# Four leading units instead of two after each sub-layer boundary, and all low parts of the weights on VectorE

## The chip, the cores and the metric

The kernel runs on one core of one Trainium2 chip. The metric is the device time of one launch in microseconds (us). A run is one execution; the time before is the median of three runs, and one more execution was profiled. The core has a matrix engine (PE, with a separate queue PEld for loading the stationary operand), VectorE (DVE), ScalarE (ACT), GpSimd (POOL) and SyncE (SP, which here only issues DMA transfers). Each engine works off its own instructions in order and waits on semaphores for the others.

## The reference

One layer of a hybrid decoder is applied to 512 prompt tokens and 8 single-token samples, 520 token columns in all, with a model width of 1024. Norms cross all three sub-layers:

```
x = x + 0.5 * rmsnorm(swiglu(rmsnorm(x, g1), gate1, up1, down1), post1)     # first feed-forward, hidden 2816
m, states  = token_mixer(rmsnorm(x, gm), ...)                                # mixer
x = x + rmsnorm(m, postm)
x = x + 0.5 * rmsnorm(swiglu(rmsnorm(x, g2), gate2, up2, down2), post2)     # second feed-forward
swiglu(x)  = (silu(x @ gate) * (x @ up)) @ down
token_mixer: proj = h @ w_in; retention branch (4 heads), gated delta branch (4 heads, short conv of width 4,
             chunks of 64, a triangular solve per chunk), y = sig(gr)*(o_r @ w_r) + sig(gg)*(o_g @ w_g); y @ w_out
```

Outputs are the new x of prompt and samples and the new retention, delta and conv states.

## The kernel before, in words

Activations are kept transposed: a tile `x[k]` holds 128 channels (k = 0 to 7) by 520 tokens. Every matmul takes a 128x128 piece of a weight as stationary operand and 260 tokens (a half, `HALVES`) as moving operand. Full float32 accuracy comes from three passes over float32r parts (`passes`, L298 to L300): high part of the weight times high part of the activation, high times low (`xl`), low times high. A weight's high part `whi` is a cast by ACT (L258), its low part `wlo` the difference raw minus `whi` (L259). `split_x` does the same for activations: ACT writes the high part (L389), DVE the low part (L390), both in a tile `xhl`.

A **unit** is the weight of one output tile of 128 channels: 8 pieces k. A unit over both halves is 8 x 3 x 2 = 48 matmuls; it is one product `product`. Plain pairs of the feed-forwards (`g` for gate, `u` for up) are two units each, `PLAIN` = 3 of them in each feed-forward; the other 19 pairs (m from 3 to 21) are computed in seven products of half depth and half the tokens each (`seven`, tile `sv`), 84 matmuls where a plain pair has 96, from combined weights (`s1`, `s3`, `a22` with sums made by DMA) and combined activations (`token_factors`). Their order is the table `stream`. `hidden` turns a plain pair into a hidden tile: `t` = g * r on DVE (L617), silu on ACT (L621), product on DVE, and the split of it.

The program is written in the order in which the engines execute it. Side tasks are Python generators (`spawn`); each `yield n` gives the main stream of PE work n steps (`tick`) before the task emits its next instructions. So a number in a `yield` sets how many matmuls stand on PE between two steps of a chain. `next_unit` hands out the next split weight and calls `prefetch`, which emits the split of units to come (two ahead) as buffers come free; `hold` stops that while x is being prepared.

At a boundary between sub-layers the following happens. The last output tile `dn` of the sub-layer is done half by half (`down`, `staged`). `post` for a half takes the sum of squares (PE `ss`, L360), the inverse root (POOL `pow`, L355), spreads it over the partitions (PE `rb`, L366), then for each k DVE makes `t` = y * rb (L492), POOL adds it to x (L494), ACT and DVE split x. So the next sub-layer's PE work can start on half 0 as soon as the first `xhl` is there. The inverse root of the new x (`pre_rms`) needs both halves; ACT squares x (L407), DVE adds the squares over k (`add_squares`, L435), then `inverse_rms` makes `ss`, `rs`, and `rb` for both halves. It isn't needed by the products themselves, which are scaled by r after the matmul, but by what reads them.

`two_first` takes the first two units together: at half 0, k by k, both units, then the same at half 1; the half 0 result of the first is copied out of PSUM (`early`). Then come units 2 and 3 over both halves each. The first units of the mixer are GAB (gates), CK, CQ, CV of head 0, of the second feed-forward the gate and up of pairs 0 and 1. `urgent` units (number 2) are split in four pieces; `on_pool` units, and every odd unit in the mixer while `share_split` is set, have their low part made on POOL rather than DVE (30 in all).

## Time and profile before

| | us |
| --- | --- |
| median of three runs | 1298.24 |
| lowest and highest | 1297.49, 1301.72 |
| the profiled execution's own time | 1299.34 |
| its span (first to last instruction) | 1297.3 |
| PE busy, mean granted clock | 1233.3, 0.962 |
| DVE, ACT, POOL busy | 866.5, 547.0, 317.2 |

What lies outside the span is 2.0 us. In the profile, L numbers are lines of the kernel before; an entry such as `[2.18 <-ACT whi L258]` behind an instruction says that its engine was idle for 2.18 us before it and what released it. Times of places are counted from the start of the span: the first feed-forward ends and the mixer begins at about 379 us, the second feed-forward begins at about 892 us.

### The profile page before, as it was taken

What the parts mean: (1) busy time and instruction counts of PE and PEld (TensorE: products, weight loads), DVE (VectorE), ACT (ScalarE), POOL (GpSimd) and SP (SyncE); (2) the same over time, 40 slices, a digit from 0 to 9 for tenths busy, and PEclk for the clock granted to TensorE, in tenths of its full rate; (3) what the DMA queues carried; (4) which work ended last, traced back from release to release, by engine and by line L of the source; (5) the groups of instructions that cost most, each with busy time, mean ns of one, the idle gap of its engine ahead of it and who ended that gap; (6) DMA issues with size and microseconds to landing.
All of it is one profiled execution on the core that took longest, in us unless ns stands there. A gap on an engine that the chain in (4) does not pass through costs nothing.

```text
span 1297.3 us, 25497 instructions
## 1 busy us (share of the span) xinstructions
PE 1233.3 (95%) x10061; PEld 1219.7 (94%) x10061; DVE 866.5 (67%) x1911; ACT 547.0 (42%) x1127; POOL 317.2 (24%) x410
## 2 busy tenths in 40 slices
PE   8899999999998997999999999998889999999995
PEld 7899999999988997989999999998889999999995
DVE  8888888642254887877687655446768887862334
ACT  6566655522233553212333343323546655542220
POOL 4111211000024359227512333403311111100003
PEclk8999999999997999899999999997889999999997
DMA  5677777243321233232333564321377777634321
GB/s 172 170 182 195 177 185 178 86 156 92 97 62 53 95 101 89 71 101 97 106 133 111 178 205 136 126 82 50 119 192 183 180 196 182 147 90 156 90 74 66
DMA packets 77127, 167.38 MB, mean 129 GB/s; under 512 B 14544, under 2 KB 20016, under 8 KB 77008
## 3 DMA queue, kind: packets, MB, share of 16 engines
q1 hardware_dynamic: 64432, 140.95, 33.9%
q0 software_dynamic: 12576, 24.81, 10.9%
q8 instruction: 79, 1.29, 0.4%
q14 instruction: 40, 0.33, 0.1%
HBM read 156.03 MB, written 9.70 MB: 128 GB/s over the span
## 4 chain that ended last, share of the span: by engine, by line
PE 71%; DVE 11%; POOL 5%; issue 4%; DMA 4%; ACT 3%; SPq 1%; POOLq 0%; ACTq 0%; DVEq 0%
PE sv L298 10%; PE sv L299 10%; PE sv L300 10%; PE dn L299 7%; PE dn L298 7%; PE dn L300 7%; PE p L298 4%; PE p L300 4%; PE p L299 4%; DVE wlo L259 2%; DMA s<-gu_in 2%; DVE cv L1048 1%; PE br L298 1%; PE br L299 1%; PE br L300 1%
## 5 line engine op out<-in xcount | busy, mean ns | idle before, releaser
L298 PE MATMUL p<-xhl,whi 128*128 128x260 f32 x784 | 237.5, 303 | 2.2 <-ACT whi L258 2.2
L300 PE MATMUL p<-xhl,wlo 128*128 128x260 f32 x784 | 227.8, 291 | 1.8 <-DVE wlo L259 1.0
L299 PE MATMUL p<-xhl,whi 128*128 128x260 f32 x784 | 228.3, 291 | 0.7 <-DVE xhl L390 0.6
L299 PE MATMUL dn<-hl,whi 128*128 128x260 f32 x704 | 199.6, 283 | 3.3 <-DVE hl L606 3.3
L298 PE MATMUL dn<-hh,whi 128*128 128x260 f32 x704 | 199.5, 283 | 0.0
L300 PE MATMUL dn<-hh,wlo 128*128 128x260 f32 x704 | 198.8, 282 | 0.0
L298 PE MATMUL sv<-th,w 128*128 128x260 f32 x608 | 173.2, 285 | 4.4 <-ACT u L638 4.3
L299 PE MATMUL sv<-tl,w 128*128 128x260 f32 x608 | 172.9, 284 | 0.0
L300 PE MATMUL sv<-th,w 128*128 128x260 f32 x608 | 172.9, 284 | 0.0
L298 PEld LDWEIGHTS p<-xhl,whi 128*128 128x128 f32 x784 | 154.5, 197 | 3.1 <-ACT whi L258 2.4
L259 DVE TENSOR_TENSOR wlo<-raw,whi 128x1024 fp32r<-128x1024 f32 (+2 forms) x107 | 116.4, 1105 | 60.4 <-ACT whi L258 60.0
L300 PEld LDWEIGHTS p<-xhl,wlo 128*128 128x128 f32 x784 | 154.1, 197 | 2.3 <-DVE wlo L259 1.2
L299 PEld LDWEIGHTS p<-xhl,whi 128*128 128x128 f32 x784 | 154.3, 197 | 1.6 <-DVE xhl L390 1.1
L258 ACT CAST whi<-raw 128x1024 fp32r<-128x1024 f32 (+2 forms) x137 | 126.7, 943 | 65.5 <-DMA raw<-dn_in 55.2
L218 POOL DMA_DIRECT2D s<-gu_in x76 | 67.1, 954 | 322.6 <-DMA s<-gu_in 149.1
L277 DVE TENSOR_TENSOR w<-s,w 128x512 fp32r<-128x512 f32 x152 | 104.5, 689 | 53.2 <-ACT w L276 52.1
L299 PEld LDWEIGHTS dn<-hl,whi 128*128 128x128 f32 x704 | 132.6, 188 | 4.1 <-DVE hl L606 4.1
L298 PE MATMUL sv<-xhl,w 128*128 128x260 f32 x456 | 129.4, 284 | 4.2 <-DVE t L617 4.2
L300 PEld LDWEIGHTS dn<-hh,wlo 128*128 128x128 f32 x704 | 132.6, 188 | 0.0
L298 PEld LDWEIGHTS dn<-hh,whi 128*128 128x128 f32 x704 | 132.6, 188 | 0.0
L299 PE MATMUL sv<-xhl,w 128*128 128x260 f32 x456 | 129.0, 283 | 0.0
L300 PE MATMUL sv<-xhl,w 128*128 128x260 f32 x456 | 128.9, 283 | 0.0
(362 smaller groups left out, 2990.8 us busy)
## 6 DMA issues: line engine op xcount, KB each, us to landing
raw<-gu_in SPq DMA_DIRECT2D x49, 512.0 KB, 3.7
raw<-win_in SPq DMA_DIRECT2D x49, 512.0 KB, 3.5
s<-gu_in SPq DMA_DIRECT2D x76, 256.0 KB, 4.2
s<-gu_in POOLq DMA_DIRECT2D x76, 256.0 KB, 4.8
raw<-dn_in SPq DMA_DIRECT2D x32, 448.0 KB, 3.5
a<-gu_in SPq DMA_DIRECT2D x38, 256.0 KB, 4.6
raw<-dn_in SPq DMA_DIRECT2D x16, 512.0 KB, 3.6
x<-x SPq DMA_DIRECT2D x16, 260.0 KB, 6.3
```

What stands on the lines that cost most here:

```text
L218: self.nc.gpsimd.dma_start(out=out, in_=term, accum_op=ALU.add)
L258: self.nc.scalar.copy(hi[:, ks], t[:, ks])
L259: eng.tensor_tensor(lo[:, ks], t[:, ks], hi[:, ks].bitcast(F32), ALU.subtract)
L277: nc.vector.tensor_tensor(w[:, 1], t[i], w[:, 0].bitcast(F32), ALU.subtract)
L298: mm(ps, hi[:, k, :], xh, start=first, stop=False, skip_group_check=more)
L299: mm(ps, hi[:, k, :], xl, start=False, stop=False, skip_group_check=more)
L300: mm(ps, lo[:, k, :], xh, start=False, stop=last, skip_group_check=more)
L1048: nc.vector.scalar_tensor_tensor(out=acc, in0=cin[:, j : j + SEQ], scalar=w[:, j : j + 1], in1=acc, op0=ALU.mult, op1=ALU.add)
```

## The change

The diff does five things.

1. In mixer and second feed-forward, four units lead (`first_units` with groups (0,1) and (2,3)) where `two_first` had two: half 0 of units 0 and 1 interleaved over k, half 0 of units 2 and 3, then the same at half 1. The half 0 results of all are copied out by ACT. The first feed-forward keeps two units, one behind the other.
2. All low parts are made on DVE; `on_pool`, `share_split` and `urgent` are gone.
3. In `post`, the split of unit 1 is emitted behind the second `t` of half 0, and those of units 2 and 3 behind the last `xhl` of half 0. The squares are added once, 520 wide, after half 1 (seven additions in place of fourteen half as wide), `inverse_rms` waits for the first group's half 1 and one step, and its spread comes four steps behind the root instead of two.
4. The second feed-forward has four plain pairs, so one pair fewer in sevens.
5. In both feed-forwards the `hidden` of the last plain pair is spawned when the stream is at its fourth product (n == 3), no longer ahead of the stream.

On PE, around the start of the mixer, the order before was the following (rows are the first matmul of each turn of a tile; `p` are the projection's PSUM tiles, and the operand in the middle tells the unit, `whi_4692` unit 0, `whi_4912` unit 1, `whi_5101` unit 2):

```order
L298 MATMUL p_4908<-xhl_4837,whi_4692 128x260 [waits Activation_49]
L298 MATMUL p_4918<-xhl_4837,whi_4912 128x260 [waits Activation_49]
...
L360 MATMUL ss_4939<-ones,acc_638_3487 65x1 x4
...
L366 MATMUL rb_4977<-cst,rs_4946 128x65 [waits Pool_49]
...
L298 MATMUL p_5020<-xhl_5003,whi_4692 128x260 [waits Activation_49]
L298 MATMUL p_5024<-xhl_5003,whi_4912 128x260 [waits PE_49]
...
L298 MATMUL p_5127<-xhl_4837,whi_5101 128x260 [waits Activation_49]
L298 MATMUL p_5128<-xhl_5003,whi_5101 128x260 [waits PE_49]
L360 MATMUL ss_5135<-ones,sq_4820 65x1 [waits PE_49]
```

And it is now (`whi_4692`, `whi_4826`, `whi_4971`, `whi_4977` are units 0 to 3):

```order
L294 MATMUL p_4908<-xhl_4849,whi_4692 128x260 [waits Activation_49]
L295 MATMUL p_4908<-xhl_4849,whi_4692 128x260 [waits DVE_49]
L296 MATMUL p_4908<-xhl_4849,wlo_4693 128x260
L294 MATMUL p_4912<-xhl_4849,whi_4826 128x260
...
L294 MATMUL p_5020<-xhl_4849,whi_4971 128x260 [waits Activation_49]
L294 MATMUL p_5024<-xhl_4849,whi_4977 128x260 [waits PE_49,Activation_49]
...
L294 MATMUL p_5123<-xhl_5015,whi_4692 128x260 [waits Activation_49]
...
L356 MATMUL ss_5187<-ones,sq_4832 65x1 [waits DVE_49]
```

Half 0 of units 2 and 3 (`p_5020`, `p_5024`) has moved ahead of the first matmul of half 1 (`p_5123`), and the sum of squares `ss_5187` stands 60 matmuls further from it: 48 of half 1 of units 0 and 1, and 12 of units 2 and 3.

On DVE at the same place, before and then now (`wlo` of unit 1 ahead of the fifth `t` to after the second, `t` and `xhl` are the pieces of half 0; `sq` the sums of the squares):

```order
L390 SCALAR_TENSOR_TENSOR xhl_4889<-x_3862,vec,xhl_4889 128x260 [waits Activation_49]
L401 TENSOR_TENSOR acc_638_3487<-acc_638_3487,s_4893 128x260 [waits Activation_49]
L512 TENSOR_SCALAR y_4758<-dn_4763,gh 128x260
L259 TENSOR_TENSOR wlo_4913<-raw_4683,whi_4912 128x1024 [waits DMAHW0_49,Activation_49]
...
L390 SCALAR_TENSOR_TENSOR xhl_4954<-x_3865,vec,xhl_4954 128x260 [waits Activation_49]
L435 TENSOR_TENSOR sq_4820<-sq_4820,sq_4821 128x260
```

```order
L474 TENSOR_TENSOR t_4823<-y_3849,rb_4809 128x260
L255 TENSOR_TENSOR wlo_4827<-raw_4683,whi_4826 128x1024 [waits DMAHW0_49,Activation_49]
L474 TENSOR_TENSOR t_4846<-y_4026,rb_4809 128x260 [waits Pool_49]
L384 SCALAR_TENSOR_TENSOR xhl_4849<-x_3858,vec,xhl_4849 128x260 [waits Activation_49]
...
L384 SCALAR_TENSOR_TENSOR xhl_4961<-x_3865,vec,xhl_4961 128x260 [waits Activation_49]
L255 TENSOR_TENSOR wlo_4972<-raw_4696,whi_4971 128x1024 [waits DMAHW1_49,Activation_49]
L255 TENSOR_TENSOR wlo_4978<-raw_4830,whi_4977 128x1024 [waits DMAHW2_49,Activation_49]
```

The low part of unit 1 has moved ahead of the first `xhl`, and where the first seven additions of squares stood, the low parts of units 2 and 3 stand now.

On ACT at the start of the first feed-forward's stream (`s_775` is silu of the last plain pair, `u` and `q` copies of the stream's first results out of PSUM), before and now:

```order
L276 CAST w_139_761<-s_120_625 128x512 [waits PE_49]
L621 ACTIVATE s_775<-t_765 128x260 [waits DVE_49,Activation_49]
L621 ACTIVATE s_776<-t_766 128x260 [waits DVE_49,Activation_49]
L638 COPY u_779<-sv_751 128x260 [waits PE_49]
```

```order
L272 CAST w_139_761<-s_120_625 128x512 [waits PE_49]
L640 COPY u_770<-sv_751 128x260 [waits PE_49]
L272 CAST w_143_787<-s_142_785 128x512 [waits DVE_49,Activation_49]
L643 COPY q_790<-sv_772 128x260 [waits PE_49]
L272 CAST w_145_804<-a_105_535 128x512 [waits DMAHW2_49,Activation_49]
L646 COPY u_807<-sv_751 128x260 [waits PE_49]
L272 CAST w_150_826<-raw_532 128x512 [waits Activation_49]
L623 ACTIVATE s_831<-t_816 128x260 [waits DVE_49,Activation_49]
```

The two silu have moved behind three copies and three casts.

The diff:

```diff
@@ -37,7 +37,7 @@
 RAW_BUFS, SPLIT_BUFS, AHEAD = 2, 9, 2
 SUM_LAG = 6
 SLOTS = 68
-PLAIN = {1: 3, 2: 3}
+PLAIN = {1: 3, 2: 4}
 SPLIT_H = 10
 
 
@@ -127,9 +127,6 @@
         self.first_of = {}
         for j, g in enumerate(self.group):
             self.first_of.setdefault(g, j)
-        kinds = [u[0] for u in self.unit_list]
-        self.on_pool = {kinds.index("win") + n for n in (3, 4)} | {kinds.index("gu2") + 3}
-        self.urgent = {kinds.index("win") + 2, kinds.index("gu2") + 2}
         self.loaded = {}
         self.split_done = {}
         self.raw_next = self.split_next = self.use_next = 0
@@ -140,8 +137,8 @@
         self.rooted = False
         self.ahead = 0
         self.tasks = []
-        self.share_split = False
         self.hold = False
+        self.leads = 0
         self.now = 0
 
 
@@ -237,7 +234,7 @@
                 self.split_seven(j)
             else:
                 nk = self.unit_list[j][3] - self.unit_list[j][2]
-                self.split(j, [slice(z, z + 2) for z in range(0, nk, 2)] if j in self.urgent else [slice(0, nk)])
+                self.split(j, [slice(0, nk)])
             self.load_to(self.split_next)
 
     def started(self, j):
@@ -253,10 +250,9 @@
             self.started(j)
         t = self.loaded[self.group[j]]
         hi, lo = self.split_done[j]
-        eng = self.nc.gpsimd if j in self.on_pool or self.share_split and j % 2 else self.nc.vector
         for ks in parts:
             self.nc.scalar.copy(hi[:, ks], t[:, ks])
-            eng.tensor_tensor(lo[:, ks], t[:, ks], hi[:, ks].bitcast(F32), ALU.subtract)
+            self.nc.vector.tensor_tensor(lo[:, ks], t[:, ks], hi[:, ks].bitcast(F32), ALU.subtract)
 
     def split_seven(self, j):
 
@@ -368,13 +364,11 @@
             )
         return pb[:, 0:HC]
 
-    def rstd(self, acc, scale, wait, plus, meanwhile=None):
+    def rstd(self, acc, scale, wait, plus):
 
         ps = self.bank("ss")
         self.sums(ps, acc, PIECES)
         _, r = self.root(ps, PIECES, scale, plus)
-        if meanwhile is not None:
-            meanwhile()
         yield wait
         return self.spread(r)
 
@@ -417,22 +411,12 @@
                 while len(xs[hf]) <= k:
                     yield 1
                 self.square(k, hf, nc.scalar)
-            if hf == 0:
-
-                while not self.clear:
-                    yield 1
-                self.add_squares(0)
-        self.prefetch(True, 1)
-        self.add_squares(1)
-        yield 2
+        for k in range(1, KD):
+            nc.vector.tensor_tensor(sq[0], sq[0], sq[k], ALU.add)
+        while not self.leads:
+            yield 1
+        yield 1
         yield from self.inverse_rms(sq[0], r, plus)
-        self.hold = False
-
-    def add_squares(self, hf):
-        c0, n = HALVES[hf]
-        acc = self.sq[0][:, c0 : c0 + n]
-        for k in range(1, KD):
-            self.nc.vector.tensor_tensor(acc, acc, self.sq[k][:, c0 : c0 + n], ALU.add)
 
     def inverse_rms(self, acc, r, plus):
         nc = self.nc
@@ -442,7 +426,8 @@
         if plus is not None:
             nc.vector.tensor_scalar(plus[0:PW], m[0:PW], EPS, None, ALU.mult)
         self.rooted = True
-        yield 2
+        self.hold = False
+        yield 4
         out = self.wk.tile([P, TOK], F32, tag="rb", name=self.name("rb"), bufs=1)
         for hf, (c0, n) in enumerate(HALVES):
             pb = self.spread(s[:, hf * PIECES : (hf + 1) * PIECES])
@@ -460,11 +445,8 @@
         c0, n = HALVES[hf]
         cs = slice(c0, c0 + n)
         self.hold = self.hold_sums = gnext is not None
-        yield 1
-        meanwhile = (lambda: self.clear.append(1)) if hf else (lambda: self.prefetch(True, 1))
-        r2 = yield from self.rstd(
-            acc, 1.0 / D, 2 if gnext is None else 3, plus and plus[0:PW, hf * PIECES : (hf + 1) * PIECES], gnext is not None and meanwhile or None
-        )
+        yield 1 if gnext is None else 2
+        r2 = yield from self.rstd(acc, 1.0 / D, 2 if gnext is None else 3, plus and plus[0:PW, hf * PIECES : (hf + 1) * PIECES])
         if gnext is None:
             r2s = self.work("u", n)
             nc.scalar.copy(r2s, r2)
@@ -483,7 +465,7 @@
             return
         if not hf:
             self.rooted = False
-            self.clear = []
+            self.leads = 0
             self.spawn(self.pre_rms(xs, r, plus_next))
...
             if k >= lag:
                 xs[hf].append(self.split_x(k - lag, hf, gnext))
+            if not hf and k == 1:
+                self.prefetch(True, 1)
             yield 1
+        if not hf:
+            self.prefetch(True, 2)
 
 
     def down(self, xin, pieces, gpost, gnext, held, plus=None, plus_next=None, x_from=None):
@@ -531,19 +517,35 @@
         self.staged([job] * held, sum(pieces), xin, "dn", lambda j, hf, ps: evac(KD - held + j, hf, ps), False)
         return xs, r
 
-    def two_first(self, xs, name, by_k):
-
...
-        self.staged([lambda: [(self.next_unit(), range(KD))]] * 2, KD, xs, name, done, by_k)
+    def first_units(self, xs, name, groups):
+
+
+        n = sum(len(g) for g in groups)
+        ws, banks = [None] * n, [[None, None] for _ in range(n)]
+        early = [self.slot("early") for _ in range(n // 2)]
+        for hf, (c0, cols) in enumerate(HALVES):
+            for group in groups:
+                ps = {}
+                for k in range(KD):
+                    for j in group:
+                        if ws[j] is None:
+                            ws[j] = self.next_unit()
+                        while len(xs[hf]) <= k:
+                            self.tick()
+                        if j not in ps:
+                            ps[j] = self.dbank(name, cols)
+                        self.passes(ws[j], k, xs[hf][k], ps[j], k == 0, k == KD - 1)
+                    if len(group) > 1 or k % 2:
+                        self.tick()
+                for j in group:
+                    banks[j][hf] = ps[j]
+                    if hf:
+                        self.release()
+                    else:
+                        banks[j][0] = early[j // 2][:, j % 2 * HC : j % 2 * HC + cols]
+                        self.nc.scalar.copy(banks[j][0], ps[j])
+                if hf:
+                    self.leads += 1
         return banks
 
     def token_factors(self, xs, gcol, F):
@@ -680,15 +682,24 @@
             return banks, at
 
         self.spawn(self.token_factors(xs, gpre, F))
-        self.spawn(hidden(*self.two_first(xs, "g", x_from is not self.a["xT"])))
-        for m in range(1, plain):
+        lead = self.first_units(xs, "g", ((0,), (1,)) if x_from is self.a["xT"] else ((0, 1), (2, 3)))
+
+        def leads():
+            for j in range(0, len(lead), 2):
+                yield from hidden(*lead[j : j + 2])
+
+        self.spawn(leads())
+        for m in range(len(lead) // 2, plain):
             pg = self.product([(self.next_unit(), range(KD))], xs, "g")
             pu = self.product([(self.next_unit(), range(KD))], xs, "u")
-            self.spawn(hidden(pg, pu))
+            if m < plain - 1:
+                self.spawn(hidden(pg, pu))
         while r[0] is None or r[1] is None:
             self.tick()
         pairs = {}
-        for m, i in stream(plain):
+        for n, (m, i) in enumerate(stream(plain)):
+            if n == 3:
+                self.spawn(hidden(pg, pu))
             if m not in pairs:
                 pairs[m] = pair(m)
             banks, at = pairs[m]
@@ -825,30 +836,18 @@
         self.turn = 0
         self.gcol = None
         self.dec_done = set()
-        tiles, gate, lead = {}, {}, {}
+        tiles, gate, lead = {}, {}, []
 
         def project(kind, h):
-            if kind == GAB:
-                lead[GAB, 0], lead[CK, 0] = self.two_first(xs, "p", True)
-                return
-            if (kind, h) == (CK, 0):
-                return
-            ps = self.product([(self.next_unit(), range(KD))], xs, "p")
             if lead:
-                lead[kind, h] = ps
-                if len(lead) < 4:
-                    return
-                while r[0] is None or r[1] is None:
-                    self.tick()
-                self.spawn(self.gates(self.gate_rows(lead[GAB, 0])))
-                for kind in (CK, CQ):
-                    tiles[kind] = self.conv(lead[kind, 0], kind, 0)
-                lead.clear()
-                self.share_split = True
-                kind = CV
+                ps = lead.pop(0)
+            else:
+                ps = self.product([(self.next_unit(), range(KD))], xs, "p")
             if (kind, h) == (CK, 1):
                 self.spawn(positions())
-            if kind in (CQ, CK, CV):
+            if kind == GAB:
+                self.spawn(self.gates(self.gate_rows(ps)))
+            elif kind in (CQ, CK, CV):
                 tiles[kind] = self.conv(ps, kind, h)
                 if kind == CV:
                     self.spawn(self.gdn_head(h, tiles[CQ], tiles[CK], tiles[CV]))
@@ -878,6 +877,9 @@
 
                 self.spawn(tanh())
 
+        lead += self.first_units(xs, "p", ((0, 1), (2, 3)))
+        while r[0] is None or r[1] is None:
+            self.tick()
         for kind, h in proj_order()[: -2 * KD]:
             project(kind, h)
         yx, part = [[], []], []
...
```

More of the change, by code (lines that the diff above doesn't have):

```diff
@@ L532, in down @@
         return xs, r
-    def two_first(self, xs, name, by_k):
-        banks = [[None, None], [None, None]]
-        early = self.slot("early")
-        def done(j, hf, ps):
-            if j == 0:
-                c0, n = HALVES[hf]
-                self.nc.scalar.copy(early[:, c0 : c0 + n], ps)
-                ps = early[:, c0 : c0 + n]
-            banks[j][hf] = ps
-        self.staged([lambda: [(self.next_unit(), range(KD))]] * 2, KD, xs, name, done, by_k)
+    def first_units(self, xs, name, groups):
[25 more added lines that the diff above has]
+                    self.leads += 1
         return banks
```

1 line of the change is left out of this document (removed).

## The prediction

> **What bounds the kernel now.** I read the page first: engines and slices.
>
> ```profile
> PE 1233.3 (95%) x10061; PEld 1219.7 (94%) x10061; DVE 866.5 (67%) x1911; ACT 547.0 (42%) x1127; POOL 317.2 (24%) x410
> ...
> PEclk8999999999997999899999999997889999999997
> ```
>
> PE, busy 95% of the span, is the bound nearly everywhere. The clock row has a digit per slice of 32.4 us; behind the start it dips in the slices from 389, 519 and 876 to 940 us. There is time to win only where PE idles, and where its clock is below 1. So I asked for windows around the two boundaries (columns: stretch, length, busy us and count of PE, PEld, DVE, ACT, POOL, then granted clock, DMA share, GB/s):
>
> ```profile
> 379.15:429.70 50.55, 43.99 (x294) 42.44 (x293) 30.39 (x70) 18.59 (x42) 18.36 (x19) 0.80 0.17 53
> 379.80:383.20 3.40, 0.51 (x2) 0.30 (x2) 3.40 (x6) 3.40 (x8) 1.71 (x2) 0.98 0.00 0
> 383.00:390.00 7.00, 6.62 (x35) 6.62 (x35) 5.42 (x13) 1.06 (x3) 2.39 (x2) 0.51 0.25 77
> 400.10:403.50 3.40, 1.91 (x20) 1.82 (x19) 3.26 (x9) 1.12 (x4) 0.00 (x0) 1.00 0.29 42
> 403.50:417.20 13.70, 12.53 (x62) 12.53 (x63) 1.64 (x5) 2.27 (x3) 6.34 (x3) 0.50 0.17 68
> 411.50:429.70 18.20, 18.20 (x132) 18.02 (x132) 9.17 (x23) 4.28 (x6) 5.26 (x5) 0.84 0.27 88
> 429.70:480.00 50.30, 50.22 (x423) 49.96 (x422) 42.29 (x98) 31.94 (x81) 24.86 (x27) 1.00 0.35 107
> 480.00:580.00 100.00, 86.77 (x688) 84.53 (x686) 83.04 (x237) 29.10 (x69) 52.28 (x89) 0.91 0.29 88
> 891.80:938.90 47.10, 39.32 (x243) 37.59 (x242) 35.30 (x75) 23.41 (x52) 16.93 (x17) 0.75 0.25 80
> 895.00:908.70 13.70, 12.21 (x58) 11.91 (x59) 8.12 (x18) 2.67 (x6) 4.05 (x6) 0.50 0.10 40
> 922.30:932.60 10.30, 9.59 (x46) 9.33 (x45) 7.68 (x12) 5.30 (x11) 3.34 (x2) 0.50 0.17 58
> 938.90:954.60 15.70, 11.54 (x97) 11.33 (x95) 8.87 (x16) 4.51 (x9) 2.39 (x3) 0.95 0.86 235
> ```
>
> At full clock a matmul takes 50.22 / 423 = 0.119 us, so a unit of 48 takes 5.7 and four take 22.8. The first four units of the mixer take 50.55 us, those of the second feed-forward 47.1: 28 and 24 us more than their matmuls. Half of that is clock: 20.7 us at half speed in the mixer (10.3 lost), 24.0 in the feed-forward (12.0 lost). Each such stretch follows a few us in which PE was little busy (0.51 of 3.40, 1.91 of 3.40). What those stalls are, the waits of PE say (line, releaser, us in total, times, longest):
>
> ```profile
> PE cs L1370 <- DVE gsq L1482: 5.6, 1, 5.6
> PE ss L360 <- DVE sq L435: 5.3, 2, 2.7
> PE sv L298 <- ACT u L638: 4.3, 2, 3.4
> PE sv L298 <- DVE t L617: 4.2, 1, 4.2
> PE g L298 <- ACT whi L258: 3.4, 1, 3.4
> PE rb L366 <- POOL rs L355: 3.1, 3, 1.3
> PE p L298 <- ACT whi L258: 2.2, 1, 2.2
> ```
>
> Unit 1's split comes late (`whi`, 2.2 and 3.4), the sum of squares stands on the path (`sq`, twice 2.7).
>
> **Lead of the mixer.** The change gives PE 48 matmuls between the halves that need no new x, and puts unit 1's split ahead of the pieces. The pieces of x come at one per 0.90 us (xhl at 378.53, the next at 379.43):
>
> ```profile
> 378.53 0.60 DVE L390 SCALAR_TENSOR_TENSOR xhl<-x,vec,xhl 128x260 fp32r<-128x260 f32 x1
> 379.43 0.60 DVE L390 SCALAR_TENSOR_TENSOR xhl<-x,vec,xhl 128x260 fp32r<-128x260 f32 x1
> 950.90 0.69 DVE L571 TENSOR_TENSOR tl<-ta,th 128x520 fp32r<-128x520 f32 x1
> 405.99 1.64 POOL L355 TENSOR_TENSOR rs<-ms,mhalf 65x8 f32<-65x8 f32 x1 [7.11 <-DVE ms L351]
> L259 DVE TENSOR_TENSOR wlo<-raw,whi 128x1024 fp32r<-128x1024 f32 x59 | 73.3, 1242 | 13.4 <-ACT whi L258 13.2
> ```
>
> My walk: unit 1's `wlo` ahead of the first xhl, 1.2; half 0 of units 0 and 1 paced by x, 8 x 0.90 plus the last six matmuls, 7.9; a wait on the sums of half 1 and on `rb`, up to 2.7 together (rows above: 1.3 for the longest `rb`, and an estimate of the same again); half 0 of units 2 and 3, 5.7; by then x of half 1 is ahead of PE, so its 48 matmuls run dense, 5.7, and 12 of units 2 and 3, 1.4. The seven additions are now 520 wide, 0.69 each by the nearest row of that width, 4.8 in all, and start behind the last xhl. From `rb` DVE has two `wlo` (2.5), three `t` and a split (some 2) to the first piece of half 1, and 7 x 0.90 to the last: 10.8; PE has 12 + 48 + 60 matmuls, 14.3, to `ss`, 3.5 more, less some 0.3 to get going. 4.8 - 3.2 is a wait of 1.6. Then 36 matmuls, 4.3, and the two spreads, 2.0. Sum 32.5 against 50.55: 18 us. The root (1.64 on POOL and some 0.5 around it) has 24 matmuls, 2.9 us, in front of `rb`, and hides; without them it would be 2.1 on the path. From this I take 2 off, since a wait of 1.6 or the `rb` wait may still put a stretch at half clock: a short one, such as 383 to 390, costs 3.5, and I weigh it at a little over one half. **16**, bounds 11 (two short stretches) and 20 (`rb` and `ss` waits gone).
>
> **Low parts on VectorE.** POOL loses its 30, DVE gets 30 at 1.24:
>
> ```profile
> L259 POOL TENSOR_TENSOR wlo<-raw,whi 128x1024 fp32r<-128x1024 f32 x30 | 73.3, 2444 | 43.7 <-ACT whi L258 30.7 <-PE pS L1223 12.8
> L1048 DVE SCALAR_TENSOR_TENSOR cv<-cin,vec,cv 128x512 f32<-128x512 f32 x36 | 35.8, 994 | 10.4 <-ACT cv L1046 9.6
> 425.81 2.33 DVE L1048 SCALAR_TENSOR_TENSOR cv<-cin,vec,cv 128x512 f32<-128x512 f32 x3 [0.72 <-ACT cv L1046]
> 429.61 4.34 DVE L1048 SCALAR_TENSOR_TENSOR cv<-cin,vec,cv 128x512 f32<-128x512 f32 x3 [0.72 <-ACT cv L1046]
> 430.59 2.81 POOL L259 TENSOR_TENSOR wlo<-raw,whi 128x1024 fp32r<-128x1024 f32 x1 [1.53 <-ACT whi L258]
> 504.40 2.40 POOL L259 TENSOR_TENSOR wlo<-raw,whi 128x1024 fp32r<-128x1024 f32 x1
> 512.38 1.63 POOL L1150 TENSOR_TENSOR rr<-se,mhalf 128x8 f32<-128x8 f32 x1
> 514.04 0.17 DVE L1159 TENSOR_TENSOR cols<-se,rr 128x4 f32<-128x4 f32 x1 [1.71 <-POOL rr L1150]
> ```
>
> Added to DVE: 30 x 1.24 = 37 us. Given back: while a split runs on POOL, DVE operations stand still. Three `cv` take 2.33 without and 4.34 beside one, 2.0 more; 30 of these would be 60, the `cv` group alone shows 36 x (0.994 - 0.777) = 8 (0.777 is 2.33 / 3). I take 25, so DVE gets 12 more of net work, spread over 470 us of mixer. In the Trainium skill, "SBUF — State Buffer", section "Who interferes with whom", a DVE operation with two SBUF inputs and a GpSimd operation that reads SBUF exclude each other for the whole instruction; by that up to 73 us would come back and DVE would gain 36; the 2.0 per split above agrees in kind, not in size.
>
> DVE is busy 42.29 of 50.30 us from 429.7 and 83.04 of 100 from 480, so 12 fit into the gaps if the chain isn't there at that moment. What is on the path: POOL's queue. `rr` at 512.38 stands behind the split at 504.40 and small pieces of the solve; DVE's `cols` waits 1.71 for it, and PE's longest wait, 5.6 on `gsq`, is behind `cols` on DVE. Without the split POOL is 2.4 earlier there, so of 5.6 some 2 to 5 go. Against it: DVE made the convolutions of units 1 and 2 while PE was still busy with unit 3, and now they come after it: 9.17 us of DVE work from 411.5 to 429.7 is then still to do when PE turns to the fifth unit. This lag has 50.30 - 42.29 = 8.0 us of free DVE to go into up to 480. Together I take **1** off for the inside of the mixer, bounds 6 off and 8 on.
>
> **Start of the second feed-forward.** The same walk gives 31.4 there (the sums wait 2.1 in place of 1.6 and the entry is shorter) against 47.1: 15.7. One plain pair more costs 12 matmuls, 1.4. At 954.66 PE waited 4.2 for `t`, and this isn't a matter of order: DMA is 0.86 busy from 938.9, and the sevens' weights arrive, are cast and summed just ahead. The lead now ends 15 us earlier, the additional pair covers 96 matmuls, 11.4, of it; I leave the stall at 4.5, 0.3 more. The second wait on `u`, 4.3 - 3.4 = 0.9, goes, as below. A stretch at half clock behind `ss` or behind the stall is likelier than in the mixer, 2.5 off. 15.7 - 1.4 - 0.3 + 0.9 - 2.5 = **12**, bounds 6 and 15.
>
> **The deferred `hidden`.** In the first stream:
>
> ```profile
> 55.58 1.14 ACT L276 CAST w<-s 128x512 fp32r<-128x512 f32 x2 [2.64 <-DMA s<-gu_in]
> 57.44 0.76 DVE L617 TENSOR_TENSOR t<-g,rb 128x260 f32<-128x260 f32 x2
> 57.96 0.76 ACT L621 ACTIVATE s<-t 128x260 f32<-128x260 f32 x2 [1.24 <-DVE t L617]
> 58.62 0.36 ACT L638 COPY u<-sv 128x260 f32<-128x260 f32 x1
> 59.03 0.58 PE L298 MATMUL sv<-th,w 128*128 128x260 f32 x1 [3.39 <-ACT u L638]
> ```
>
> The copy `u` that frees PE's bank stands on ACT behind two silu, which wait for `t`, which DVE makes behind sums that wait for a DMA until 55.58. With `hidden` out of the way `u` may run when the casts end, 56.72, not 58.62: **2** off (bounds 1 and 3.4). Late next is the DMA itself. The silu run later beside PE work; nothing reads that hidden tile before the down projection.
>
> **Sum.** 16 + 1 + 12 + 2 = 31 off the profiled 1299.34 (span 1297.3 and 2.0 around it): 1268.3. The median of the runs shown is 1.1 below the profiled run; the forecast for a median is 1267.
>
> **Rivals.**
>
> *The clock falls at both boundaries as before.* Stalls remain in the lead (`rb`, `ss`), and they might give full stretches again. For: PE was 1.91 of 3.40 busy at 400.1, and that was enough. Against: 48 dense matmuls stand right before. Price: two long stretches of 13.7 and 10.3 and a short one of 7.0 lose 15.5, of which 4.5 is in the sum, and the waits that carry them some 7 more: +18, 1285.
>
> *No drop at all.* If only a wait of about a whole 3.4 us lowers the clock, waits of 1.6 and 2.1 leave it. Price: the 4.5 come back, 1262. Against: 1.91 of 3.40 busy lowered it. In the Trainium skill, "TensorE: Matmul & The Clock Gate", section "HAM oscillation — how this bites in real kernels", the rule is no idle gap above about 3.4 us; by it the wait of 2.7 on `sq` couldn't have lowered the clock, and this trace differs at 403.5 (0.50).
>
> *The second feed-forward waits for its weights.* The lead and the plain pairs run out 15.7 earlier, and the stall at 954.66 grows by what the transfers don't keep up with. For: DMA at 0.86 there. Against: 0.25 from 891.8, and 11.4 us more cover. Price: 12 of the gain, 1279.
>
> *Slower: DVE becomes the bound of the mixer.* Place: 429.7 to 580. Added there and after are 37, only 8 return (the `cv` group alone), and 9 come with the lead's convolutions: 38. The gaps of DVE from 429.7 to 580 are 8.0 + 17.0 = 25, most in front of a chain that PE waits for. It decides if less than about 5 of the 38 find a gap: then 33 on and the inside's 1 off falls away, 1301. At half of that it's a smaller gain.
>
> **How the numbers follow.** Forecast 0.40, clock as before 0.18, no drop 0.18, weights 0.12, DVE bound 0.12, of which 0.08 end slower and 0.04 within 0.3%. A kernel like this can be told from no change at 0.3%, 3.9 us. Faster 0.88, same 0.04, slower 0.08. The range goes from the best bounds (20 + 6 + 15 + 3.4 = 44 off, 1254) to just above the clock rival, 1288; it leaves the DVE rival out.
>
> **What would show it.** In the profile after: the lead of the mixer some 33 to 36 us long and that of the second feed-forward 31 to 35, with granted clock above 0.9 in both; no wait of PE on `whi` L254 at a boundary; `ss` waits at 1.5 to 2.7; POOL about 244 busy, with no `wlo`; `cv` at a mean near 780 ns; the wait on `gsq` under 4; `sv` waits on `u` at about 1.5 in the first stream; 4 to 5 at the second stream's start. I'm wrong if PE's idle from 430 to 700 rises above what it was by more than 10, or if the lead of either boundary stays above 42.

## The result, and the profile after

The changed kernel takes 1267.07 us (median of four, 1265.27 to 1271.86), the kernel before 1298.35 (four, 1297.49 to 1301.72). The ratio is 0.976, 95% interval 0.9727 to 0.9793. The forecast was 1267, with 1254 to 1288.

The page of the changed kernel, engines and clock row, answers to the first lines of the prediction:

```profile
PE 1214.7 (96%) x10073; PEld 1203.5 (95%) x10073; DVE 864.6 (68%) x1911; ACT 538.5 (43%) x1117; POOL 255.9 (20%) x378
...
PEclk8999999999999899999999999999989999999997
```

PE is 18.6 us less busy with 12 matmuls more: what went is time at half clock (mean granted clock 0.962, now 0.977), in which the same matmul counts longer (0.42 us at 400.9, where the clock is halved, 0.28 just before). DVE, which took over 30 low parts, is 1.9 us less busy than before, where 12 more were expected. Where the clock row dipped in the slices from 389, from 519 and from 876 to 940 us, two shallow dips are left, in the slices from 411 and from 916 us.

The leads in windows of the changed kernel (columns as in the prediction): the first row is the mixer's four leading units, the second what follows up to the first branch product (the inside of the mixer), the third the four units of the second feed-forward.

```profile
375.37:408.28 32.91, 29.60 (x242) 28.86 (x241) 24.69 (x48) 17.01 (x40) 15.14 (x16) 0.95 0.28 87
408.28:682.79 274.51, 263.41 (x2224) 258.84 (x2222) 221.62 (x672) 102.57 (x241) 103.61 (x198) 0.97 0.33 103
869.34:901.00 31.66, 29.48 (x241) 28.74 (x240) 27.36 (x52) 18.29 (x42) 14.21 (x15) 0.95 0.18 60
```

The prediction sets 50.55 us against the first row, but that isn't the same piece of work. Its row ends at 429.70, with the end of the fifth unit, and has 294 matmuls on PE, where the row above has 242. Cut at the first matmul of the fifth unit, as above, the kernel before had:

```profile
379.15:423.54 44.39, 37.83 (x242) 36.46 (x241) 25.78 (x57) 17.02 (x39) 17.99 (x17) 0.77 0.19 60
423.54:705.18 281.64, 265.21 (x2223) 260.04 (x2222) 223.80 (x652) 102.12 (x240) 132.77 (x213) 0.96 0.32 100
```

So the mixer's lead went from 44.39 to 32.91, at a clock of 0.95 against 0.77, and the inside from 281.64 to 274.51. The four units of the second feed-forward, where the prediction's row does hold four, are through in about 31.7 against 47.1, at 0.95 against 0.75. The waits of PE:

```profile
PE sv L294 <- DVE t L619: 4.6, 1, 4.6
PE ss L356 <- DVE acc L395: 3.6, 3, 1.8
PE cs L1371 <- DVE gsq L1483: 3.2, 1, 3.2
PE sv L294 <- ACT u L640: 3.2, 2, 2.5
PE rb L362 <- POOL rs L351: 2.5, 2, 1.3
PE ss L356 <- DVE sq L415: 1.4, 2, 1.2
```

The waits on `whi` of unit 1 (2.2 and 3.4) are gone, that on the squares is 1.4 in all where it was 5.3, and the first stream's wait on `u` is 2.5 where it was 3.4. The stall at the start of the second stream is there as before, 4.6 (4.2).

By stages of the two profiled executions, each from the start of a stage's first matmul on PE to the next: the first feed-forward is 3.8 shorter (mixer's start at 379.15, now 375.37), the mixer's lead 11.5, the inside of the mixer 7.1, the part from the first branch product to the second feed-forward 0.1, the second feed-forward 11.4. But for rounding, that is the 33.8 by which the span is shorter (1297.3, now 1263.5).

### The profile page after: what moved, and what is told of

Its sections match the earlier page's. It is cut to its first block, busy times and chain, and to the rows that moved or that the text cites. A ratio compares the mean times of both kernels' runs of the same rounds, so it can differ in the third digit from the quotient of the medians.

```text
span 1263.5 us, 25461 instructions
## 1 busy us (share of the span) xinstructions
PE 1214.7 (96%) x10073; PEld 1203.5 (95%) x10073; DVE 864.6 (68%) x1911; ACT 538.5 (43%) x1117; POOL 255.9 (20%) x378
## 4 chain that ended last, share of the span: by engine, by line
PE 72%; DVE 13%; DMA 4%; issue 3%; ACT 3%; POOL 3%; SPq 0%; DVEq 0%; ACTq 0%; POOLq 0%
PE sv L294 9%; PE sv L295 9%; PE sv L296 9%; PE dn L295 7%; PE dn L294 7%; PE dn L296 7%; PE p L294 5%; PE p L295 5%; PE p L296 5%; DMA s<-gu_in 3%; DVE wlo L255 2%; PE br L294 1%; PE br L295 1%; PE br L296 1%; DVE cv L1049 1%
## 5 line engine op out<-in xcount | busy, mean ns | idle before, releaser
L294 PE MATMUL p<-xhl,whi 128*128 128x260 f32 x784 | 234.5, 299 | 0.0
L295 PE MATMUL p<-xhl,whi 128*128 128x260 f32 x784 | 224.8, 287 | 0.0
L296 PE MATMUL p<-xhl,wlo 128*128 128x260 f32 x784 | 224.4, 286 | 0.0
L255 DVE TENSOR_TENSOR wlo<-raw,whi 128x1024 fp32r<-128x1024 f32 (+2 forms) x133 | 156.8, 1192 | 56.9 <-ACT whi L254 56.7
L294 PE MATMUL sv<-th,w 128*128 128x260 f32 x592 | 169.0, 285 | 3.4 <-ACT u L640 3.2
L296 PE MATMUL sv<-th,w 128*128 128x260 f32 x592 | 168.3, 284 | 0.0
L295 PE MATMUL sv<-tl,w 128*128 128x260 f32 x592 | 168.1, 284 | 0.0
L294 PEld LDWEIGHTS p<-xhl,whi 128*128 128x128 f32 x784 | 151.4, 193 | 0.7
L295 PEld LDWEIGHTS p<-xhl,whi 128*128 128x128 f32 x784 | 151.6, 193 | 0.1
L296 PEld LDWEIGHTS p<-xhl,wlo 128*128 128x128 f32 x784 | 151.1, 193 | 0.0
L273 DVE TENSOR_TENSOR w<-s,w 128x512 fp32r<-128x512 f32 x148 | 101.4, 689 | 52.7 <-ACT w L272 51.0
L294 PE MATMUL sv<-xhl,w 128*128 128x260 f32 x444 | 126.2, 284 | 5.2 <-DVE t L619 4.6
L295 PE MATMUL sv<-xhl,w 128*128 128x260 f32 x444 | 125.7, 283 | 0.0
L296 PE MATMUL sv<-xhl,w 128*128 128x260 f32 x444 | 125.4, 282 | 0.0
```

What stands on the lines that cost most here:

```text
L255: self.nc.vector.tensor_tensor(lo[:, ks], t[:, ks], hi[:, ks].bitcast(F32), ALU.subtract)
L273: nc.vector.tensor_tensor(w[:, 1], t[i], w[:, 0].bitcast(F32), ALU.subtract)
L294: mm(ps, hi[:, k, :], xh, start=first, stop=False, skip_group_check=more)
L295: mm(ps, hi[:, k, :], xl, start=False, stop=False, skip_group_check=more)
L296: mm(ps, lo[:, k, :], xh, start=False, stop=last, skip_group_check=more)
```

## The experiments

Each comparison is with the kernel before on the same chip. The change itself was timed twice, 0.976 and 0.9746, and its variants are read against these two. The intervals of the ratios are 0.3 to 0.7% wide, 4 to 9 us, so several variants can't be told from the change by their time alone; the stage that was edited then has to decide.

**All low parts back on GpSimd inside the mixer.** The edit, in the changed kernel:

```diff
+        eng = self.nc.gpsimd if self.share_split and j % 2 else self.nc.vector
-            self.nc.vector.tensor_tensor(lo[:, ks], ...)
+            eng.tensor_tensor(lo[:, ks], ...)
     # share_split is set behind the four leading units and cleared ahead of the mixer's down projection
```

> The changed kernel, but inside the mixer (behind the four leading units) every second unit's low part is made on GpSimd again, as before the change (27 splits). The theory of the prediction: what goes to VectorE and what comes back nearly cancel, the inside of the mixer gains about 1 from the move; expected 1268, between 1264 and 1272, GpSimd busy near 325 us, VectorE busy about 10 less. Rival A: GpSimd's queue was the bound of the inside and moving the splits off it is worth 5 or more: 1272 to 1277. Rival B: the added work on VectorE costs, and four leading units alone would be better: 1259 to 1263.

Measured: 1272.42, ratio 0.9786 (0.976 to 0.9812), so 3 to 5 us slower than the change, with intervals that overlap. It lies at the edge between the theory and rival A. The place tells more than the time. The stretch from the first `gt` (the gates' transposes) to the first branch product, in the kernel before, in the change and in this run:

```profile
427.22:705.18 277.96, 261.53 (x2192) 256.50 (x2192) 220.91 (x645) 101.40 (x239) 132.59 (x212) 0.96 0.33 101
```
```profile
411.96:682.79 270.83, 259.73 (x2193) 255.29 (x2192) 218.73 (x665) 101.85 (x240) 103.42 (x197) 0.97 0.34 104
```
```profile
413.74:692.12 278.38, 260.81 (x2192) 255.68 (x2192) 222.92 (x649) 102.12 (x240) 132.97 (x213) 0.96 0.33 101
```

With the low parts on GpSimd the stretch is 278, with or without four leading units; with them on VectorE it is 270.8. In the change VectorE is 4.2 us less busy in it (218.73 against 222.92) with 16 operations more: what comes back is more than what goes there. The other profiles agree. Eight of the change and its variants have four leading units in the mixer and no such load on GpSimd, and their stretch takes between 268.65 and 272.11 (the two rows below, from the runs with two leading units in the second feed-forward and with filler); in the kernel before with filler, where GpSimd has its load, it takes 277.2.

```profile
411.63:680.28 268.65, 260.22 (x2192) 255.47 (x2192) 218.40 (x665) 101.87 (x240) 102.67 (x197) 0.97 0.34 105
411.89:684.00 272.11, 259.67 (x2218) 254.94 (x2218) 218.41 (x665) 101.92 (x240) 103.09 (x197) 0.98 0.33 104
```

Two signs were missed: GpSimd was busy 310.6 us in all, where 325 was expected, and VectorE 2.6 less than in the change (862.0 against 864.6), where 10 was.

**The kernel before with all low parts on VectorE.** The edit:

```diff
-        eng = self.nc.gpsimd if j in self.on_pool or self.share_split and j % 2 else self.nc.vector
+        eng = self.nc.vector
```

> The kernel before, with every low part made on VectorE and nothing else changed. The theory of the prediction: about 1 off, 1297, between 1292 and 1302; VectorE busy some 12 us more than before. Rival A (GpSimd's queue was the bound of the inside): 1288 to 1293, and the wait on the gsq row under 4. Rival B (VectorE is overloaded by it): 1303 or more.

Measured: 1285.49 against 1301.08, ratio 0.9894 (0.986 to 0.9928): some 14 off, ten times what the prediction gave it, and more than rival A. This one line wins nearly half of what the whole change wins. The same stretch:

```profile
424.02:692.01 267.99, 259.98 (x2193) 255.32 (x2193) 218.01 (x662) 101.82 (x240) 102.81 (x197) 0.97 0.35 105
```

10.0 come off there. VectorE's `cv` had a mean of 994 ns; here it has 817:

```profile
L1048 DVE SCALAR_TENSOR_TENSOR cv<-cin,vec,cv 128x512 f32<-128x512 f32 x36 | 29.4, 817 | 10.5 <-ACT cv L1046 9.6
```

VectorE's whole busy time rises from 866.5 to 871.6, by 5, for 37 us of added work: 32 came back, where the prediction took 25. The mixer's lead is 5.3 shorter too in this profile: the wait of 2.66 on the squares stands in it as before, but the clock didn't fall behind it (row in the last section). Whether that is the edit's doing isn't shown.

**GpSimd's queue kept busy with something else.** The changed kernel, with memsets where the low parts were:

```diff
+        if self.busy_pool and j % 2:
+            for _ in range(10):
+                self.nc.gpsimd.memset(self.scrap, 0.0)      # 128x192
```

> The changed kernel, with all low parts on VectorE, but with ten memsets of a scratch tile on GpSimd (about 2.5 us together) at every second unit of the mixer, where the kernel before had a low part there (27 times). They occupy GpSimd's queue as the low parts did, and read nothing. Theory that the low parts on GpSimd cost by its in-order queue (rr and the solve's pieces stand behind them): the wait on gsq is near 5.6 again and the time is as with the low parts on GpSimd inside the mixer, 1271 to 1274. Rival that they cost by holding VectorE's operations: cv stays near 0.8 us and the time is the change's, 1265 to 1269.

Measured: 1270.44, ratio 0.9789 (0.9766 to 0.9811), 4 to 6 slower than the change, though the intervals still touch. Windows of the same stretch, the memsets, and the longest wait of PE:

```profile
415.55:692.64 277.09, 261.52 (x2192) 256.72 (x2192) 217.22 (x665) 101.92 (x240) 142.51 (x367) 0.96 0.34 102
...
L256 POOL MEMSET scrap<- 128x192 f32 x270 | 69.9, 259 | 14.0
...
L1056 DVE SCALAR_TENSOR_TENSOR cv<-cin,vec,cv 128x512 f32<-128x512 f32 x36 | 27.6, 767 | 10.4 <-ACT cv L1054 9.6
...
PE cs L1378 <- DVE gsq L1490: 7.4, 1, 7.4
```

The 70 us of memsets cost the stretch 6.3 (5.0 against the longest of the eight), nearly as much as the 27 low parts (7.6), though `cv` at 767 ns is not held at all. So what the low parts cost there is mainly their place in GpSimd's in-order queue. Which of the operations behind them (`rr`, the pieces of the solve) matters most was not tested. That the low parts also hold VectorE's operations is seen (994 against 817 ns), but the memsets come to nearly the same price without it. The wait on `gsq` isn't a sure sign: with a load on GpSimd it was 5.6 to 7.4, in nine of the ten profiles without one 2.0 to 4.4, but in the tenth (x stored later) 5.7.

**Two leading units in the mixer.** The edit in the changed kernel:

```diff
-        lead += self.first_units(xs, "p", ((0, 1), (2, 3)))
+        lead += self.first_units(xs, "p", ((0, 1),))
+        for _ in range(2):
+            lead.append(self.product([(self.next_unit(), range(KD))], xs, "p"))
```

> The changed kernel with two leading units in the mixer; units 2 and 3 follow as whole products, as before the change, and all else (unit 1's early split, squares added once, low parts on VectorE, four leading in the second feed-forward) as changed. The theory of the prediction: the 48 matmuls between the halves hide the waits on rb and x of half 1 and keep the clock up; without them PE is paced by x in half 1 too and the wait on ss is near 3 instead of 1.2, the lead is 40 to 46 us instead of 32.8: 1274 to 1281. Rival: what won the lead is unit 1's early split alone, and the number of leading units is worth 3 or less: 1267 to 1270.

Measured: 1268.03, ratio 0.9751 (0.973 to 0.9772); the change beside it 1266.8, 0.9746 (0.9723 to 0.9769). The time went as the rival said. The two rows, from the first product to the first `gt` and from there to the first branch product, first this run and then the change timed beside it:

```profile
376.73:420.63 43.90, 37.28 (x273) 35.77 (x271) 31.29 (x64) 17.87 (x41) 15.50 (x19) 0.88 0.22 65
420.63:684.91 264.28, 256.84 (x2192) 252.25 (x2192) 214.96 (x655) 101.10 (x239) 103.55 (x196) 0.98 0.35 107
```
```profile
376.78:413.37 36.59, 33.28 (x272) 32.42 (x271) 27.59 (x55) 17.75 (x41) 15.34 (x17) 0.95 0.26 79
413.37:682.25 268.88, 258.22 (x2192) 253.62 (x2192) 218.81 (x665) 101.99 (x240) 102.73 (x197) 0.97 0.34 105
```

The theory's mechanism is there: the lead is 7.3 longer, at a clock of 0.88. The rival's reason is not: unit 1's early split alone didn't win the lead, which at 43.90 is no shorter than the 42.81 of the kernel before with all low parts on VectorE, where unit 1's split is late. But of what four units win in the lead, the inside gives much back: it takes 4.6 more in the change's second profile than here, 6.5 more in its first. VectorE does 3.9 us less work in it here (214.96 against 218.81), which it did under the longer lead; that the chain behind therefore starts nearer to PE is likely, but was not tested. The net worth of four leading units in the mixer is within what the timing can tell.

**Two leading units in the second feed-forward.** The same edit there, `((0, 1), (2, 3))` to `((0, 1),)`.

> The changed kernel with two leading units in the second feed-forward; units 2 and 3 follow as whole products. In the mixer the same edit made the lead 7.3 us longer and the part behind it 6 shorter, +1.2 in all. Theory: here the lead also gets some 7 longer, and since no chain of VectorE stands behind it that could take it back, the time is 1271 to 1275. Rival: the stall at the start of the second stream, 4.6 to 5.0, is the arrival of weights that are asked for by the same units, and takes most of it back: 1266 to 1269.

Measured: 1270.48, ratio 0.9789 (0.9772 to 0.9806), 4 to 6 more than the change; between the two, nearer to the theory. The interval overlaps with that of the change's first timing, not of its second. From its first product to the start of the stream, here and in the change (its second and its first profile):

```profile
866.85:933.70 66.85, 58.47 (x434) 56.69 (x433) 47.67 (x91) 31.42 (x66) 17.80 (x19) 0.89 0.43 125
...
PE ss L356 <- DVE sq L415: 4.1, 2, 2.9
...
PE sv L294 <- DVE t L619: 3.2, 1, 3.2
```
```profile
868.83:931.23 62.40, 55.45 (x434) 54.73 (x433) 47.53 (x91) 32.20 (x68) 17.78 (x19) 0.92 0.44 133
869.34:928.85 59.51, 52.72 (x434) 51.80 (x433) 47.78 (x91) 31.99 (x68) 17.78 (x19) 0.95 0.46 140
```

The lead up to the stream is 4.5 to 7.3 longer. One wait on the squares is 2.9, near the 2.7 of the kernel before, and the stall in front of the stream takes back 1.4 to 1.8 (3.2 in place of 4.6 and 5.0).

**Filler on PE in the kernel before.** The edit: 10 or 16 matmuls of constants ahead of unit 1's first, 12 ahead of the sum of squares.

```diff
+    def fill(self, ps, n):
+        for _ in range(n):
+            self.nc.tensor.matmul(ps[:, 0:P], self.ones, self.ones, start=True, stop=True)
...
+                    if by_k and j == 1 and not hf:
+                        self.fill(ps[j], 10 if name == "p" else 16)
...
+        if self.x_done:
+            self.fill(ps[:, 256:384], 12)
         self.sums(ps, acc, 2 * PIECES)
```

> The kernel before, with matmuls of constants on PE in front of the two late steps at each boundary: 10 (mixer) or 16 (second feed-forward) of 128x128 ahead of unit 1's first, and 12 ahead of the sum of squares; they add work, take no wait away, and lie in time in which PE idles. Theory that about half of the leads' excess is clock: the granted clock stays at 1 through most of both leads (0.80 and 0.75 before), 12 to 20 us come off: 1278 to 1287. Rival: the waits alone set the time, the clock is a symptom: 1296 to 1301.

Measured: 1288.26 against 1299.97, ratio 0.991 (0.9891 to 0.993): 11.7 off by adding work and taking no wait away, just short of the theory's 12 to 20 and far from the rival. The two leads, from the first product to `gt` and to the stream, and the 7 us, 3.9 behind the lead's start, that were at 0.51 in the kernel before; then the two leads of the kernel before:

```profile
381.23:423.22 41.99, 39.88 (x316) 37.93 (x315) 26.99 (x62) 17.52 (x40) 17.96 (x18) 0.96 0.20 64
887.03:943.71 56.68, 47.45 (x394) 45.69 (x393) 44.88 (x90) 28.00 (x61) 19.80 (x19) 0.98 0.47 131
385.08:392.08 7.00, 6.61 (x59) 6.61 (x59) 6.17 (x15) 1.05 (x3) 2.53 (x3) 1.00 0.24 75
```
```profile
379.15:427.22 48.07, 41.51 (x272) 40.00 (x271) 28.67 (x64) 17.74 (x40) 18.18 (x18) 0.79 0.18 56
891.82:954.66 62.84, 50.84 (x339) 48.93 (x337) 44.21 (x90) 27.98 (x61) 19.32 (x19) 0.80 0.40 118
```

What unit 1 waits for comes as late as before: its first matmul in the mixer starts 2.7 us behind the first of unit 0 in both profiles. So 12.2 us of these leads were the price of the clock, although the stall at the second stream grew (7.3, row `sv` on `t`, in place of 4.2).

**Filler in the changed kernel.** The same, ahead of the sums at both boundaries (4, 6, 8, 6), the gates' sums (5) and `gsq`'s (8).

> The changed kernel with matmuls of constants on PE ahead of the sums of squares at both boundaries (4, 6, 8, 6), of the gates' sums (5) and of the delta branch's sum gsq (8), in idle time of PE. Theory that low use of PE lowers the granted clock: some of the stretches at half clock behind these places (one to three windows of 3.4 us each) go, 3 to 8 off: 1259 to 1264. Rival: the stretches move to other places or the filler costs what it saves: 1265 to 1269.

Measured: 1262.88 (1261.50 to 1267.95), ratio 0.9736 (0.9711 to 0.9761). The leads run at a clock of 1.00 and 0.99:

```profile
376.68:411.89 35.21, 34.01 (x292) 33.26 (x291) 27.56 (x55) 17.72 (x41) 15.31 (x17) 1.00 0.29 82
870.56:930.52 59.96, 54.29 (x463) 53.39 (x461) 47.78 (x91) 32.01 (x68) 17.79 (x19) 0.99 0.45 137
```

They are 1.4 and 2.4 shorter than in the change's second run, but no shorter than the best without filler: 35.23 at a clock of 1.00 in the mixer (the run with two leading units in the second feed-forward, whose code is the change's up to there) and 59.51 in the change's first profile. The median is in the theory's range, but the interval of the ratio contains both of the change's ratios: whether it is faster is open.

**Three, and five, plain pairs in the second feed-forward.** `PLAIN = {1: 3, 2: 3}` and `{1: 3, 2: 5}` in the changed kernel.

> The changed kernel with three plain pairs in the second feed-forward as before, not four. The theory of the prediction: 12 matmuls fewer are worth 1.4, but the stream of sevens starts 11.4 us earlier and its weights are late by a part of that, so the stall at its start grows from 4.6 to between 6 and 12: 1268 to 1273. Rival: the weights come when the program asks for them and the stall is no longer than with four pairs, 1265.5 or a little less.

> The changed kernel with five plain pairs in the second feed-forward. Theory: the stall at the start of the second stream is the weights' arrival, and one more pair (11.4 us of PE work in place of 10.0 in sevens) takes it from 4.6 to near 0 as the fourth took it from 10.4 to 4.6: 3 off, 1264. Rival: the stall is order, not arrival, and stays: 1.4 more, 1268.5.

Measured with three: 1271.46, ratio 0.9767 (0.9739 to 0.9795), with these waits in the streams (the last number is the longest one):

```profile
PE sv L294 <- DVE h L626: 7.6, 1, 7.6
PE sv L294 <- ACT u L640: 6.2, 3, 3.0
```

of which 3.0 of the second row belong to the first stream: some 10 at the start of the second one, against 4.6 with four. From the lead to the down projection 249.0 against 245.5 and 246.3. So the fourth pair, 1.4 us of matmuls more, pays for itself by covering transfers; in the median this can't be told from the change. With five: 1265.35, 0.9725 (0.97 to 0.9751), the wait still 3.4:

```profile
PE sv L294 <- DVE t L619: 3.4, 1, 3.4
```

The fifth pair covers 1.2 to 1.6, not 4.6, and from the lead to the down projection this profile takes 246.6, no less than with four. The stall is not arrival alone, and the time can't be told from the change's.

**x stored later.** The eight stores of x behind the first loads of the stream.

```diff
                 while len(xs[1]) < KD or r[1] is None:
                     yield 1
+            yield 44
             for k in range(KD):
                 nc.sync.dma_start(out=x2[:, k, :], in_=self.x[k])
```

> The changed kernel with the eight stores of x to memory at the start of the second feed-forward put behind the loads of the first three sevens' weights on SP's queue. Theory that the stall at the start of the second stream (4.6 to 5.0) is the arrival of the weights: these come earlier, the stall falls to 2 to 4, 1 to 3 off: 1264 to 1266. Rival: the loads wait for a raw buffer, not for bandwidth; stall and time stay, 1266.8.

Measured: 1268.65 (1261.83 to 1272.19), ratio 0.9767 (0.9733 to 0.9801). The stall is 3.8, but its time spreads over 10 us and from the lead to the down projection this profile takes 249.3. The time is inconclusive, but the trace speaks for the rival. The loads for the first two sevens are issued 42.4 and 50.0 us behind the lead's first product; in the change's second run, with the stores ahead of them, it is 42.4 and 50.1, and in both profiles the releaser is an operation of VectorE (`xd`, then `wlo`). So the stores don't hold these loads in the queue, and what bandwidth they take is at most some 1 us of the stall.

**`hidden` not deferred.** The edit in the changed kernel takes `n == 3` out again and spawns `hidden` for each plain pair ahead of the stream.

> The changed kernel, with the last plain pair's hidden step spawned ahead of the stream again in both feed-forwards. The theory of the prediction: the wait of PE on the copy u at the first stream's start returns from 2.5 to 3.4 and the clock stays low a little longer, and a second wait of 0.9 comes back in the second stream: 1269 to 1271. Rival: the first feed-forward got its 3.8 elsewhere (the spread of the root four steps later), and the deferral is worth less than 1: 1267 to 1268.

Measured: 1266.0, ratio 0.9738 (0.9712 to 0.9764). No loss: the rival is right in the end result. Yet at its place the step does what was said. From the landing of `s` (the first cast) to PE, in the change and without the deferral:

```profile
54.89 1.14 ACT L272 CAST w<-s 128x512 fp32r<-128x512 f32 x2 [2.51 <-DMA s<-gu_in]
55.93 0.37 ACT L640 COPY u<-sv 128x260 f32<-128x260 f32 x1
...
56.35 0.58 PE L294 MATMUL sv<-th,w 128*128 128x260 f32 x1 [2.50 <-ACT u L640]
```
```profile
55.02 1.14 ACT L272 CAST w<-s 128x512 fp32r<-128x512 f32 x2 [2.26 <-DMA s<-gu_in]
57.40 0.76 ACT L623 ACTIVATE s<-t 128x260 f32<-128x260 f32 x2 [1.24 <-DVE t L619]
58.06 0.36 ACT L640 COPY u<-sv 128x260 f32<-128x260 f32 x1
...
58.47 0.39 PE L294 MATMUL sv<-th,w 128*128 128x260 f32 x1 [4.22 <-ACT u L640]
```

1.46 against 3.45, 2.0 shorter. By the mixer's start (378.10 here; 375.37 to 379.62 in the profiles of the change and its other variants) nothing of it can be told any more.

**The change again.**

> The changed kernel as it is, beside the others on one chip: 1267 (1265 to 1272).

Measured: 1266.8 (1264.59 to 1269.85), ratio 0.9746 (0.9723 to 0.9769).

## Why the prediction was right, and where it was so by accident

The sum was 31, the medians give 31.3, the two profiled executions 34.1. The agreement is closer than that of the terms, and by luck: the mixer's lead gave 4.5 less than forecast and its inside 6 more. Term by term:

- **Lead of the mixer, 16** (bounds 11 to 20): 11.5. The walk was right: 32.5 stands at 32.91, with the wait on the squares 1.2 in place of 1.6, and the last wait on the sums of half 1 (row `acc`) 0.9 and `rb` 1.2 where 2.7 together were put. One short stretch of low clock came, as weighed. The step that failed is what the walk was taken from: "the first four units of the mixer take 50.55 us". That row holds a fifth unit; four took 44.39, so the walk was worth 11.9 and not 18, and with the 2 taken off the term would have been 10.
- **Inside of the mixer, 1** (6 off to 8 on): 7.1, past the better bound. Moving the low parts is worth 7.6 to 10.0 there: 278.38 to 270.83 with four leading units, 277.96 to 267.99 without them. The failed step is "of 5.6 some 2 to 5 go", which looked for the queue's price at one wait; beside `gsq`, other waits shrank too (`tr` on `ekd` from 2.0 to none in the list, `ks` on `S` from 2.2 to 1.3). What came back to VectorE was 32, not 25. Against it, the inside costs 4.6 to 6.5 more with four leading units than with two. The prediction saw VectorE's lag behind the four units ("this lag has 8.0 us of free DVE to go into") and let it vanish; if it is that lag, it did not.
- **Second feed-forward, 12** (6 to 15): 11.4 and, against the change's second run, 11.5. The stall was put at 4.5 and measured 4.6 and 5.0. Some 4 to 6 of the gain hang on four leading units (the run with two), some 3 by the trace on the fourth pair, which the prediction had down as a cost of 1.4 and as cover at once. The wait on the squares, put at 2.1, was 0.2.
- **Deferral, 2** (1 to 3.4): 2.0 where it acts, and not seen in the time. The first feed-forward's 3.8 is in part the time ahead of its stream (47.87 from its first matmul, now 46.06), which the prediction left at zero, and in part the landing of a transfer, which moves by about 2 us between executions of the same code (54.89 here, 56.69 in the first experiment). How much of the 3.8 is the change's isn't shown: the mixer starts at 379.15 to 381.23 in three profiles with the first feed-forward of before, at 375.37 to 379.62 in those of the change and its variants.

Of the rivals, the one that the clock falls in full again was wrong: 0.95 in both leads. The one by which it doesn't fall at all is refuted: behind a wait of 1.21 on the squares the change still has a window at half clock. The rule of the Trainium skill beside it ("TensorE: Matmul & The Clock Gate", section "HAM oscillation — how this bites in real kernels"), no idle gap above about 3.4 us, didn't keep the clock up here. The rows of the 3.5 us with the wait and of those behind it:

```profile
397.00:400.50 3.50, 2.29 (x28) 2.09 (x26) 2.36 (x4) 0.66 (x1) 0.00 (x0) 1.00 0.00 0
400.50:404.00 3.50, 3.50 (x20) 3.50 (x19) 2.45 (x3) 0.00 (x0) 2.57 (x1) 0.51 0.19 41
```

In the kernel before, the filler brought the clock back in a mixer's lead whose longest gap was 2.7 us. The rival of VectorE as the new bound was wrong in sign: low parts there relieve the chain. That the second feed-forward waits for its weights is half true: a stall of 3.2 to 5.3 remains in every profile with four or five pairs.

In the forecast of signs, the mixer's lead came out just under 33 to 36 and the waits on the squares under 1.5 to 2.7 (1.2 and 0.2). `cv` came to 811 ns for "near 780", POOL to 255.9 for "about 244" (its x additions take 938 ns now, 877 before), the wait on `u` to 2.5 for "about 1.5", which contains the transfer's landing.

What stays open: why the stall in front of the second stream doesn't go away with five pairs, what in the inside gives back part of the four units' gain, and whether filler in the changed kernel, or five pairs, beat it; their intervals overlap with the change's.

## What to carry to other kernels

Work put in front of a wait wins only if the chain behind it keeps up: see what the slower engine did under the old wait, since that work doesn't go away, and time the piece behind as well. An engine that looks idle (GpSimd at 24%) can set the pace through its in-order queue; the test is to keep the queue busy with something harmless and see whether the price stays. Price idle time of PE with the clock it costs afterwards: here filler matmuls alone were worth 0.9%. And when stages of two kernels are compared, count the work in each, since the stretch that was read as four units held five.

## What was not expected

VectorE took 30 operations of 1.24 us, 37 in all, and in the run with nothing else changed its busy time rose by 5. And the same code meets the low clock at other places from one execution to the next. In nine profiles the mixer's lead of four units has the same code. In three of them a stretch of 3.4 us at half clock lies some 25 us behind the lead's start (at 400.6 in the change's first profile), and the lead up to `gt` takes 36.6; in five it lies some 9 us behind, and the lead takes 35.3 to 35.4; in one there is none:

```profile
376.40:411.63 35.23, 31.93 (x272) 30.95 (x271) 27.57 (x55) 17.73 (x41) 15.34 (x17) 1.00 0.27 82
```

In the kernel before with all low parts on VectorE, the gaps of PE in the mixer's lead up to the squares are those of the kernel before (2.18, 1.02 and 2.66 us), but the last was followed by no stretch of low clock; its lead to the first `gt` took 42.81 at a clock of 0.92, that of before 48.07 at 0.79:

```profile
381.21:424.02 42.81, 35.90 (x272) 34.16 (x271) 29.62 (x64) 17.05 (x40) 13.31 (x16) 0.92 0.20 63
```

So between two profiles of the same code a lead can differ by 1.4 us (the mixer's) or 2.9 (the second feed-forward's, 59.51 and 62.40), and perhaps by the 5 of the last row. A stage is to be compared over several profiles.
